# A gated linear recurrence: decay factors kept as running products instead of sums of logarithms

## The chip, the cores and the metric

One core of a Trainium2 chip runs the whole program. The metric is the device time of one execution in microseconds, the median of several runs. Five instruction queues work side by side: PE (TensorE, matrix products), DVE (VectorE), ACT (ScalarE), POOL (GpSimd) and SP (SyncE, which issues the DMA transfers). Each queue runs in order; between queues there are semaphores.

## The reference

One layer on 1024 tokens of width 1024: a forgetting attention with 8 heads, beside it a gated linear recurrence (HGRN2) with 4 heads of width 128, both projected, gated, merged and normed, then a SwiGLU network and a second norm. The change touches the recurrence alone:

```python
# f = forget gate in (0, 1), per token and channel; k = 1 - f; q = silu(...); per head
def step(state, inp):                                   # one chunk of tokens
    q_i, k_i, v_i, g_i = inp                            # g = log f
    b = jnp.cumsum(g_i, axis=2)
    o_inter = jnp.einsum('bhtd,bhde->bhte', q_i * jnp.exp(b), state)
    diff = b[:, :, :, None, :] - b[:, :, None, :, :]
    decay = jnp.exp(jnp.where(incl[None, None, :, :, None], diff, -jnp.inf))
    attn = jnp.einsum('bhtd,bhtsd,bhsd->bhts', q_i, decay, k_i)
    o_intra = jnp.einsum('bhts,bhse->bhte', attn, v_i)
    b_last = b[:, :, -1:, :]
    k_dec = k_i * jnp.exp(b_last - b)
    new_state = (jnp.exp(b_last[:, :, 0, :])[..., None] * state
                 + jnp.einsum('bhsd,bhse->bhde', k_dec, v_i))
    return new_state, o_inter + o_intra
```

The decay between tokens s and t is the product of the forget gates after s up to t, channel by channel.

## The kernel before

Everything is written as calls on five queues (`sync`, `act`, `dve`, `pool`, `pe`), which a planner (class `Plan`) collects and then puts into an order: a list scheduler with costs per instruction and 36 rounds of changed ranks. So the order on each engine, over the whole kernel, follows from the calls, the planner's costs, and the pools of tiles (`BUFS`), whose slots come free when their last user is done. Wide products are made in three passes of split float32 (`mm3`: high by high, high by low, low by high), each with 512 columns.

The stages in order of time: the value projections (`v`), the query and key projections (`qk`), attention for 8 heads (up to about 300 us), the recurrence for 4 heads (`hgrn`, about 300 to 490 us), the gate products (`gs`), the branch projections and the merge (`pps`), the output projection (`oa`, `ob`), the network (`fa` to `fe`, `p`). `hgrn_project(h + 1)` (banks `bps`) and parts of the gate products (`gate_part`, banks `ge`) need nothing of the recurrence of head h and are planned into it.

In the recurrence a tile has 128 channels by 1024 tokens. The tokens lie in windows of 128, even windows in the first half of the tile and odd ones in the second, the odd ones in reversed order, so that `place(w)` finds window w. Before, per head:

- `fk` (tile `hbf`) becomes the gate f, `k` (`hk`) is 1 - f, then f becomes log f, and eight scans sum the logarithms within each window into `b` (`hbb`); `tot` holds the sums of whole windows and `dec` their exponentials.
- `diagonal` puts the products of a token with itself into `at`, the matrix of weights.
- `level(li)`, for L = 64, 32, 16, 8, 4, 2: tokens are taken in groups of 2L; the query of a later half meets the keys of the earlier half. `e` is b minus its value at the middle (tiles of `box1`), two exponentials turn it into factors, `ke` and `qe` are key and query times their factors, four matmuls per level give `lp`, and a masked copy puts `lp` into `at`.
- `neighbours` does the same for L = 1 by products and a matmul with ones (`lp_nb`).
- `states` makes `kd` (keys decayed to the end of the window) and `qeb` (queries decayed from its start), transposes `kd` (`kdt`), multiplies with the values (`up`) and runs over the windows (`st`, in a tile called `box`).
- At the end `op` sums `at` times the values and `qeb` times the states; then the norm, the gate and the store (`ob`, `ot`, `yb`).

In names such as `lp1_0` the first figure is the head (0 to 3). In the traces such numbers are left out, and every instruction has the line of one helper (L387).

Of the kernel before, what the change touches and what calls it, by code (L numbers as in the profile page):

```python
# [12 lines left out]
ALU = mybir.AluOpType  # L13
# [377 lines left out]
def trunk(ctx: ExitStack, tc, a: dict, out: bass.AP):  # L391
# [49 lines left out]
    def f(ap):  # L441
        return ap.bitcast(F32)

    def split(hi, lo, src):
        act.copy(hi, src)
        dve.tensor_sub(lo, src, f(hi))
# [433 lines left out]
                sync.dma_start(ya_d[p, i].rearrange("a d t -> (a d) t")[:, hs(g)], y)  # L880


    once = keep([P, P + 1], "once", F32R)
    raw = half("gt", "once_r")
    sync.dma_start(raw[:, :P + 1], a["once"])
    act.copy(once, raw[:, :P + 1])
    reset, ones = f(once)[:, :P], once[:, 1:]
    lmask = const("lmask", [P, 2, MASKS], U16, "mask")
    sync.dma_start(ng, a["ng"])
    sync.dma_start(lbl, a["lbl"])  # L890
# [12 lines left out]
    def place(w):  # L903
        return blk(w % 2 * 4 + w // 2)
# [26 lines left out]
    def halves(t, L):  # L931
        return t.rearrange("p (n c l) -> p c n l", c=2, l=L)

    def hgrn(h, qfg, box):
        q, fk, sg = qfg
        k = full("kb", f"hk{h}")
        b = full("kb", f"hbb{h}")
        act.activation(fk, fk, AF.Identity, scale=olb[:, h:h + 1], bias=lb[:, h:h + 1])
        pool.tensor_scalar(k, fk, -1.0, 1.0, op0=ALU.mult, op1=ALU.add)
        act.activation(fk, fk, AF.Ln)  # L940


        bw, fw = (t.rearrange("p (c j t) -> p c j t", c=2, t=P) for t in (b, fk))
        pool.memset(bw[:, 1, :, 0:1], 0.0)
        for w in range(NT):
            o = w % 2
            dve.tensor_tensor_scan(b[:, place(w)][:, o:], reset[:, :P - o], fk[:, place(w)][:, :P - o], 0.0,
                                   op0=ALU.mult, op1=ALU.add)
        tot = small([P, 4, 2], "tot", 1)
        dve.tensor_copy(tot[:, :, 0:1], bw[:, 0, :, P - 1:P])  # L950
        dve.tensor_add(tot[:, :, 1:2], bw[:, 1, :, P - 1:P], fw[:, 1, :, P - 1:P])
        dec = small([P, NT], "dec", 1)
        act.activation(dec, tot.rearrange("p j c -> p (j c)"), AF.Exp)

        at = full("pf", f"at{h}")
        qeb = full("pf", f"qeb{h}")
        kd = full("pf", f"kd{h}")
        kdt = box[:, h % 2, :]
        st = box[:, 2 + h % 2, :]

# [3 lines left out]
        def diagonal():  # L964
            kh, kl = (full("hl", f"qk{n}{h}", F32R) for n in "hl")
            dve.tensor_mul(at, q, k)
            split(kh, kl, at)
            for hf in range(2):
                dg = bank("s", f"dg{h}_{hf}")
                for r in (kh, kl):  # L970
                    mm(dg, ones, r[:, hs(hf)], start=r is kh, stop=r is kl)
                dve.tensor_mul(at[:, hs(hf)].rearrange("p (w t) -> p w t", t=P),
                               dg.rearrange("p (w t) -> p w t", t=P), ident[:, None, :].to_broadcast([P, 4, P]))

        def level(li):
            L = LEVELS[li]
            nb = S // (2 * L)
            e = box1[:, li % 4, :]
            ev = e.rearrange("p (n a l) -> p n a l", a=2, l=L)
            bv = b.rearrange("p (n t) -> p n t", t=2 * L)  # L980
            dve.tensor_sub(e.rearrange("p (n t) -> p n t", t=2 * L), bv,
                           bv[:, :, L - 1:L].to_broadcast([P, nb, 2 * L]))
            act.activation(ev[:, :, 0, :], ev[:, :, 0, :], AF.Exp, scale=-1.0)
            act.activation(ev[:, :, 1, :], ev[:, :, 1, :], AF.Exp)
            ke = take("hl", [NB], f"ke{h}_{li}")
            qe = half("ph", f"qe{h}_{li}")
            dve.tensor_mul(halves(ke, L), across(k, L), across(e, L))
            dve.tensor_mul(halves(qe, L), across(q, L, 1), across(e, L, 1))
            lp = bank("s", f"lp{h}_{li}")
            for j in range(NT // 2):  # L990
                mm(lp[:, blk(j)], ke[:, blk(j)], qe[:, blk(j)], start=True, stop=True)
            nw = 64 // L

            if li:
                m = lmask[:, :, 4 * nw - 7:8 * nw - 7, None].to_broadcast([P, 2, 4 * nw, L])
            else:
                m = lmask[:, :, :1, None].to_broadcast([P, 2, 4, L])
            dve.copy_predicated(across(at, L, 1), m, halves(lp, L))

        def neighbours():  # L1000

            low = take("hl", [2, NB], f"nb{h}", F32R)
            hi, lo = low[:, 0, :], low[:, 1, :]
            pr, e = (half("ph", f"nb{n}{h}") for n in "pe")
            b2 = b.rearrange("p (n a) -> p n a", a=2)
            dve.tensor_sub(e, b2[:, :, 1], b2[:, :, 0])
            act.activation(e, e, AF.Exp)
            def by2(t):
                return t.rearrange("p (c n l) -> p c n l", c=2, l=1)

            dve.tensor_mul(by2(pr), across(q, 1, 1), across(k, 1))
            dve.tensor_mul(pr, pr, e)
            split(hi, lo, pr)
            lp = bank("s", f"lp{h}_nb")
            for r in (hi, lo):
                mm(lp, ones, r, start=r is hi, stop=r is lo)
            dve.copy_predicated(across(at, 1, 1).rearrange("p c (j n) l -> p c j (n l)", j=4),
                                lmask[:, :, None, MASKS - 64:].to_broadcast([P, 2, 4, 64]),
                                lp.rearrange("p (c j n) -> p c j n", c=2, j=4))

        def states():

            even, odd = hs(0), hs(1)
            for j in range(4):
                for c, t in enumerate((kd, qeb)):
                    w = blk(4 * c + j)
                    act.activation(t[:, w], b[:, w], AF.Exp, bias=tot[:, j, c:c + 1], scale=-1.0)
            act.activation(kd[:, odd], b[:, odd], AF.Exp)
            act.activation(qeb[:, even], b[:, even], AF.Exp)
            dve.tensor_mul(kd, kd, k)  # L1030
            for hf in range(2):
                tp = bank("pt", f"kdt{h}_{hf}")
                m = min(4, NT - 1 - 4 * hf)
                for w in range(m):
                    tr(tp[:, blk(w)], kd[:, place(4 * hf + w)], ident)
                act.copy(kdt[:, hf * NB:hf * NB + m * P], tp[:, :m * P])
            dve.tensor_mul(qeb, qeb, q)
            for hf in range(2):
                up = bank("pt", f"up{h}_{hf}")
                ws = range(4 * hf, min(4 * hf + 4, NT - 1))  # L1040
                for w in ws:
                    mm(up[:, blk(w % 4)], kdt[:, blk(w)], V(w), start=True, stop=True)
                for w in ws:
                    if w == 0:
                        dve.tensor_copy(st[:, blk(1)], up[:, blk(0)])
                    else:
                        dve.scalar_tensor_tensor(st[:, blk(w + 1)], st[:, blk(w)], dec[:, w:w + 1], up[:, blk(w % 4)],
                                                 op0=ALU.mult, op1=ALU.add)

        diagonal()  # L1050
        for li in range(4):
            level(li)
        states()
        for li in range(4, len(LEVELS) - 1):
            level(li)
        neighbours()

        for hf in range(2):
            op = bank("pv", f"op{h}_{hf}")
            ss, rr = (lambda t: (t[:, :4], t[:, 4:]))(small([P, 8], "ss", 3, "ss"))  # L1060
            for w in range(4):
                ww = 4 * hf + w
                mm(op[:, blk(w)], at[:, place(ww)], V(ww), start=True, stop=ww == 0)
                if ww:
                    mm(op[:, blk(w)], qeb[:, place(ww)], st[:, blk(ww)], start=False, stop=True)
            ob = half("tt", f"ob{h}_{hf}")
            for w in range(4):
                act.activation(ob[:, blk(w)], op[:, blk(w)], AF.Square, accum_out=ss[:, w:w + 1])
# [832 lines left out]
def _constants():  # L1901
# [1 line left out]
    ident = np.eye(P, dtype=np.float32)  # L1903
    causal = np.where(s[None, :] > s[:, None], np.float32(BIG), np.float32(0))
    causal = np.tile(np.concatenate([causal, causal.T], axis=1), (1, NT // 2))
    once = np.ones((P, P + 1), np.float32)
    once[:, 0] = 0
# [14 lines left out]
    return {"before": -before, "ident": ident, "causal": causal, "once": once,  # L1922
            "lmask": lmask}


# [70 lines left out]
```

## Time and profile before

| | |
|---|---|
| median of 3 runs | 1412.72 us (1412.63 to 1412.78) |
| span of the profiled execution, first to last instruction | 1410.3 us |
| median less that span (the profiled execution has no other time on record) | 2.4 us |
| PE busy, of the span | 1399.7 us, 99% |
| DVE busy | 1161.6 us, 82% |
| ACT busy | 710.5 us, 50% |
| POOL busy | 87.3 us, 6% |
| granted TensorE clock | 0.999 |

The page lists busy time by engine, then the span in 40 slices (35 us each; the recurrence is about slices 8 to 13), then groups of instructions by the tile they write and the tiles they read (`out<-in`), and waits by who released whom. A float32 matmul with 128 columns stands there as two records, one with 512 columns in split form as one.

### The profile page before, as it was taken

How to read it: one execution, taken by the hardware profiler on the slowest of the kernel's cores; microseconds unless marked ns; L12 is line 12 of the kernel's file. 1: busy time of each engine (PE TensorE's matmuls, PEld its weight loads, DVE VectorE, ACT ScalarE, POOL GpSimd, SP SyncE). 2: the span in 40 equal slices, each digit the busy share in tenths (PEclk: the TensorE clock that was granted, in tenths of full speed). 3: DMA queues.
4: the chain of work that ended last, by engine and by line, in shares of the span. 5: the costliest groups of instructions: out<-in, count | busy, mean ns of one | idle time of the engine just before them, and what ended most of it. 6: DMA issues, size and time to landing. Idle time of an engine off the chain costs nothing.

```text
span 1410.3 us, 19118 instructions
## 1 busy us (share of the span) xinstructions
PE 1399.7 (99%) x6650; PEld 1162.8 (82%) x6650; DVE 1161.6 (82%) x2025; ACT 710.5 (50%) x1275; POOL 87.3 (6%) x108
## 2 busy tenths in 40 slices
PE   9999999999999999999999999999999999999997
PEld 7788888888888888888887888888888888888886
DVE  7995878899998979778998879877687976699597
ACT  5534689887687632365439842233223334434330
POOL 0000133420000000000001000000000000000001
PEclk9999999999999999999999999999999999999999
DMA  7458999811113686456644637533334336878632
GB/s 274 156 167 271 301 291 259 243 61 45 46 53 113 215 254 196 134 165 220 231 131 140 208 103 227 181 117 100 98 106 141 112 112 209 315 249 284 216 122 90
DMA packets 99503, 245.23 MB, mean 174 GB/s; under 512 B 11456, under 2 KB 12736, under 8 KB 99408
## 3 DMA queue, kind: packets, MB, share of 16 engines
q1 hardware_dynamic: 98256, 239.83, 52.2%
q0 software_dynamic: 1152, 4.19, 1.6%
q8 instruction: 52, 0.85, 0.2%
q14 instruction: 43, 0.35, 0.1%
HBM read 181.26 MB, written 62.72 MB: 173 GB/s over the span
## 4 chain that ended last, share of the span: by engine, by line
PE 79%; DVE 1%; issue 0%; DVEq 0%
PE p L387 15%; PE fb L387 12%; PE gs L387 9%; PE fc L387 8%; PE bps L387 7%; PE fa L387 5%; PE fe L387 3%; PE pps L387 3%; PE oa L387 3%; PE ob L387 2%; PE ge L387 2%; PE lp L387 2%; PE op L387 1%; PE pv L387 1%; PE pt L387 1%; PE x1t L387 0%
## 5 line engine op out<-in xcount | busy, mean ns | idle before, releaser
L387 PE MATMUL p<-dp 128*128 128x512 f32 (+1 forms) x957 | 210.0, 382 | 0.0
L387 PEld LDWEIGHTS p<-dp 128*128 128x128 f32 x957 | 175.3, 188 | 34.8
L387 PE MATMUL fc<-xs,Tp 128*128 128x512 f32 x528 | 129.1, 389 | 0.0
L387 PE MATMUL fb<-xs,Tp 128*128 128x512 f32 x528 | 127.8, 389 | 0.0
L387 ACT CAST Tp<-t 128x512 fp32r<-128x512 f32 x88 | 54.4, 620 | 128.9 <-PE fb L387 69.1
L387 PEld LDWEIGHTS fc<-xs,Tp 128*128 128x128 f32 x528 | 99.0, 188 | 20.8 <-ACT Tp L387 0.3
L387 PEld LDWEIGHTS fb<-xs,Tp 128*128 128x128 f32 x528 | 99.1, 188 | 20.6
L387 DVE TENSOR_TENSOR Tp<-t,Tp 128x512 fp32r<-128x512 f32 x88 | 60.3, 689 | 30.9 <-ACT Tp L387 30.3
L387 PE MATMUL fa<-x,Tp 128*128 128x512 f32 x336 | 81.4, 389 | 0.0
L387 PE MATMUL bps<-xl,wb_h 128*128 128x512 f32 x192 | 77.1, 402 | 0.0
L387 PE MATMUL bps<-xh,wb_h 128*128 128x512 f32 x192 | 76.6, 401 | 0.0
L387 PE MATMUL bps<-xh,wb_l 128*128 128x512 f32 x192 | 76.2, 400 | 0.0
L387 PEld LDWEIGHTS fa<-x,Tp 128*128 128x128 f32 x336 | 63.1, 188 | 13.1
L387 ACT CAST dp<-dap 128x1024 fp32r<-128x1024 f32 (+1 forms) x42 | 41.2, 980 | 58.8 <-PE p L387 35.6
L387 POOL TENSOR_TENSOR norm<-norm,few 128x1 f32<-128x1 f32 x16 | 13.3, 830 | 902.8 <-DVE norm L387 882.9
L387 DVE TENSOR_TENSOR dp<-dap,dp 128x1024 fp32r<-128x1024 f32 (+1 forms) x42 | 47.5, 1132 | 22.4 <-ACT dp L387 22.4
L387 DVE TENSOR_TENSOR tl<-pt,th 128x512 fp32r<-128x512 f32 (+1 forms) x96 | 52.1, 551 | 8.9 <-PE pv L387 4.2
L387 PE MATMUL fb<-x,Tp 128*128 128x512 f32 x240 | 57.8, 389 | 0.0
L387 ACT CAST th<-pt 128x512 fp32r<-128x512 f32 (+1 forms) x96 | 45.4, 477 | 16.5 <-PE pt L387 9.8
L387 PEld LDWEIGHTS fb<-x,Tp 128*128 128x128 f32 x240 | 45.0, 188 | 9.4
L387 DVE TENSOR_TENSOR u<-fb,p 128x512 f32<-128x512 f32 x40 | 27.6, 690 | 22.7 <-PE fb L387 22.5
L387 PEld LDWEIGHTS bps<-xl,wb_h 128*128 128x128 f32 x192 | 36.2, 189 | 6.3
(1006 smaller groups left out, 3594.8 us busy)
## 6 DMA issues: line engine op xcount, KB each, us to landing
dbp<-in_w_fo SPq DMA_DIRECT2D x45, 512.0 KB, 4.8
dap<-a_d SPq DMA_DIRECT2D x35, 512.0 KB, 4.8
wg_r<-in_w_ff SPq DMA_DIRECT2D x22, 512.0 KB, 3.9
wu_r<-in_w_ff SPq DMA_DIRECT2D x22, 512.0 KB, 3.9
a_d<-ar SPq DMA_DIRECT2D x42, 256.0 KB, 3.0
wop_r<-in_w_o SPq DMA_DIRECT2D x18, 512.0 KB, 3.7
a_d<-as SPq DMA_DIRECT2D x33, 256.0 KB, 3.5
qk_d<-qk SPq DMA_DIRECT2D x32, 256.0 KB, 4.8
```

Of the source, the lines that this page charges most:

```text
L387: getattr(q.engine, method)(*args, **kw)
```

## The change

Logarithms, sums, differences and exponentials go. For groups of L tokens G[L] holds the product of the L gates of each group; G[1] is f itself, and G[2L] is the product of neighbours in G[L] (tile `hg`). `k` and a new tile `qf` (query times f) hold key and query already multiplied with the decay inside their group of L tokens. To go from L to 2L, `grow(L)` multiplies in place the later halves of `qf` by G[L] of the earlier half, the earlier halves of `k` by G[L] of the later half, and makes G[2L]. So the levels now run from 2 tokens upwards, `neighbours` comes first and `states` last; after `grow(64)`, `k` and `qf` are what `kd` and `qeb` were, and `dec` is G[128]. `level(L)` copies the earlier halves of `k` into `ke` on ACT, and the matmuls read the later halves of `qf` where they lie, by a strided pattern (`later_half`). The constant `once` is no longer loaded; its ones come from a memset.

```diff
-    once = keep([P, P + 1], "once", F32R)
-    raw = half("gt", "once_r")
-    sync.dma_start(raw[:, :P + 1], a["once"])
-    act.copy(once, raw[:, :P + 1])
-    reset, ones = f(once)[:, :P], once[:, 1:]
+    ones = keep([P, P], "once", F32R)
+    raw = half("gt", "once_r")[:, :P]
+    dve.memset(raw, 1.0)
+    act.copy(ones, raw)
...
+    def later_half(t, L, j):
+        return bass.AP(tensor=t.tensor, offset=t.offset + L + P * j,
+                       ap=[list(t.ap[0]), [2 * L, 64 // L], [NB - L, 2], [1, L]])
+    def spread(t, L, other=0):
+        t = across(t, 1, other)
+        dims = [list(d) for d in t.ap]
+        dims[3] = [0, L]
+        return bass.AP(tensor=t.tensor, offset=t.offset, ap=dims)
...
-        act.activation(fk, fk, AF.Ln)
-        pool.memset(bw[:, 1, :, 0:1], 0.0)
-        for w in range(NT):
-            o = w % 2
-            dve.tensor_tensor_scan(b[:, place(w)][:, o:], reset[:, :P - o], fk[:, place(w)][:, :P - o], 0.0,
-                                   op0=ALU.mult, op1=ALU.add)
...
-        qeb = full("pf", f"qeb{h}")
-        kd = full("pf", f"kd{h}")
+        qf = full("pf", f"qf{h}")
+        gs = full("kb", f"hg{h}")
+        G, o = {1: fk}, 0
+        for L in LEVELS[::-1]:
+            G[2 * L] = gs[:, o:o + S // (2 * L)]
+            o += S // (2 * L)
...
             dve.tensor_mul(at, q, k)
+            dve.tensor_mul(qf, q, fk)
...
-        def level(li):
-            L = LEVELS[li]
-            e = box1[:, li % 4, :]
-            dve.tensor_sub(e.rearrange("p (n t) -> p n t", t=2 * L), bv,
-                           bv[:, :, L - 1:L].to_broadcast([P, nb, 2 * L]))
-            act.activation(ev[:, :, 0, :], ev[:, :, 0, :], AF.Exp, scale=-1.0)
-            act.activation(ev[:, :, 1, :], ev[:, :, 1, :], AF.Exp)
-            dve.tensor_mul(halves(ke, L), across(k, L), across(e, L))
-            dve.tensor_mul(halves(qe, L), across(q, L, 1), across(e, L, 1))
+        def grow(L):
+            dve.tensor_mul(across(qf, L, 1), across(qf, L, 1), spread(G[L], L))
+            dve.tensor_mul(across(k, L), across(k, L), spread(G[L], L, 1))
+            two = G[L].rearrange("p (n a) -> p n a", a=2)
+            dve.tensor_mul(G[2 * L], two[:, :, 0], two[:, :, 1])
+        def level(L):
+            act.copy(halves(ke, L), across(k, L))
...
-                mm(lp[:, blk(j)], ke[:, blk(j)], qe[:, blk(j)], start=True, stop=True)
+                mm(lp[:, blk(j)], ke[:, blk(j)], later_half(qf, L, j), start=True, stop=True)
...
         def states():
-            for j in range(4):
-                for c, t in enumerate((kd, qeb)):
-                    w = blk(4 * c + j)
-                    act.activation(t[:, w], b[:, w], AF.Exp, bias=tot[:, j, c:c + 1], scale=-1.0)
-            act.activation(kd[:, odd], b[:, odd], AF.Exp)
-            act.activation(qeb[:, even], b[:, even], AF.Exp)
-            dve.tensor_mul(kd, kd, k)
+            dec = G[P]
...
         diagonal()
-        for li in range(4):
-            level(li)
+        neighbours()
+        grow(1)
+        for L in LEVELS[-2::-1]:
+            level(L)
+            grow(L)
         states()
-        for li in range(4, len(LEVELS) - 1):
-            level(li)
-        neighbours()
```

The planner orders the new calls anew. TensorE, head 1, the first levels before, where two groups of `lp` stand close together:

```order
L387 MATMUL kdt1_0_1023<-ident_164,kd1_1006 128x128 x4
L387 MATMUL lp1_0_1013<-qe1_0_1012,ke1_0_1011 128x128 x4
L387 MATMUL bps1_2_0_1055<-xl1_69,wb1_2_h1_1053 128x512
L387 MATMUL lp1_1_1016<-qe1_1_1015,ke1_1_1014 128x128 x4
L387 MATMUL kdt1_1_1024<-ident_164,kd1_1006 128x128 x3
```

and now, where the transposes have gone to the end and ten projections stand between the first two levels:

```order
L387 MATMUL lp1_2_1002<-qf1_992,ke1_2_1001 128x128 x4
L387 MATMUL lp1_nb_1000<-nb1_998,once_190 128x512
L387 MATMUL bps1_2_0_1035<-xh0_66,wb1_2_l0_1032 128x512
L387 MATMUL bps1_2_0_1035<-xh0_66,wb1_2_h0_1031 128x512
L387 MATMUL bps1_2_0_1035<-xl0_68,wb1_2_h0_1031 128x512
L387 MATMUL bps1_2_0_1035<-xh0_66,wb1_2_l0_1032 128x512
L387 MATMUL bps1_2_0_1035<-xh1_67,wb1_2_h1_1033 128x512
L387 MATMUL bps1_2_0_1035<-xl1_69,wb1_2_h1_1033 128x512
L387 MATMUL bps1_2_0_1035<-xh1_67,wb1_2_l1_1034 128x512
L387 MATMUL bps1_2_0_1035<-xh1_67,wb1_2_h1_1033 128x512
L387 MATMUL bps1_2_0_1035<-xl1_69,wb1_2_h1_1033 128x512
L387 MATMUL bps1_2_0_1035<-xh1_67,wb1_2_l1_1034 128x512
```

The group of the second level, `lp1_4`, is the next row after this piece. On VectorE, head 1, before, `ke` and `qe` of a level are written while another level's product is taken out:

```order
L387 TENSOR_TENSOR ke1_3_1020<-hk1_1000,box1_106 128x2x32x8
L387 TENSOR_TENSOR qe1_3_1021<-hbq1_976,box1_106 128x2x32x8
L387 COPY_PREDICATED at1_1004<-lmask_192,lp1_1_1016 128x2x8x32
L387 SCALAR_TENSOR_TENSOR yb0_1_975<-ot0_1_974,few_119,hbg0_906 128x512
L387 TENSOR_TENSOR box1_106<-hbb1_1001 128x1024
L387 COPY_PREDICATED at1_1004<-lmask_192,lp1_2_1019 128x2x16x16
```

and now, at the same levels of 8 and 16 tokens, each product grows `k` or `qf` itself, between the masked copies:

```order
L387 COPY_PREDICATED at1_991<-lmask_192,lp1_4_1004 128x2x64x4
L387 TENSOR_TENSOR hk1_990<-hk1_990,hg1_993 128x2x16x16
L387 TENSOR_TENSOR qf1_992<-qf1_992,hg1_993 128x2x32x8
L387 COPY_PREDICATED at1_991<-lmask_192,lp1_8_1006 128x2x32x8
L387 TENSOR_TENSOR hk1_990<-hk1_990,hg1_993 128x2x8x32
```

So the masked copy of a level now stands between two growths in the same queue.

More of the change, by code (lines that the diff above doesn't have):

```diff
@@ L936, in hgrn @@
         k = full("kb", f"hk{h}")
-        b = full("kb", f"hbb{h}")
         act.activation(fk, fk, AF.Identity, scale=olb[:, h:h + 1], bias=lb[:, h:h + 1])
         pool.tensor_scalar(k, fk, -1.0, 1.0, op0=ALU.mult, op1=ALU.add)
-        act.activation(fk, fk, AF.Ln)
-        bw, fw = (t.rearrange("p (c j t) -> p c j t", c=2, t=P) for t in (b, fk))
-        pool.memset(bw[:, 1, :, 0:1], 0.0)
-        for w in range(NT):
-            o = w % 2
-            dve.tensor_tensor_scan(b[:, place(w)][:, o:], reset[:, :P - o], fk[:, place(w)][:, :P - o], 0.0,
-                                   op0=ALU.mult, op1=ALU.add)
[L949 to L953, printed above, removed]
-        at = full("pf", f"at{h}")
-        qeb = full("pf", f"qeb{h}")
-        kd = full("pf", f"kd{h}")
+        at = full("pf", f"at{h}")
+        qf = full("pf", f"qf{h}")
[4 more added lines that the diff above has]
+            o += S // (2 * L)
         kdt = box[:, h % 2, :]
@@ L973, in diagonal @@
                                dg.rearrange("p (w t) -> p w t", t=P), ident[:, None, :].to_broadcast([P, 4, P]))
-        def level(li):
-            L = LEVELS[li]
-            nb = S // (2 * L)
-            e = box1[:, li % 4, :]
-            ev = e.rearrange("p (n a l) -> p n a l", a=2, l=L)
-            bv = b.rearrange("p (n t) -> p n t", t=2 * L)
-            dve.tensor_sub(e.rearrange("p (n t) -> p n t", t=2 * L), bv,
-                           bv[:, :, L - 1:L].to_broadcast([P, nb, 2 * L]))
-            act.activation(ev[:, :, 0, :], ev[:, :, 0, :], AF.Exp, scale=-1.0)
-            act.activation(ev[:, :, 1, :], ev[:, :, 1, :], AF.Exp)
-            ke = take("hl", [NB], f"ke{h}_{li}")
-            qe = half("ph", f"qe{h}_{li}")
-            dve.tensor_mul(halves(ke, L), across(k, L), across(e, L))
-            dve.tensor_mul(halves(qe, L), across(q, L, 1), across(e, L, 1))
-            lp = bank("s", f"lp{h}_{li}")
+        def grow(L):
[4 more added lines that the diff above has]
+        def level(L):
+            ke = take("hl", [NB], f"ke{h}_{L}")
+            act.copy(halves(ke, L), across(k, L))
+            lp = bank("s", f"lp{h}_{L}")
             for j in range(NT // 2):
-                mm(lp[:, blk(j)], ke[:, blk(j)], qe[:, blk(j)], start=True, stop=True)
+                mm(lp[:, blk(j)], ke[:, blk(j)], later_half(qf, L, j), start=True, stop=True)
             nw = 64 // L
-            if li:
+            if L < 64:
                 m = lmask[:, :, 4 * nw - 7:8 * nw - 7, None].to_broadcast([P, 2, 4 * nw, L])
@@ L1003, in neighbours @@
             hi, lo = low[:, 0, :], low[:, 1, :]
[L1004 to L1007, printed above, removed]
+            pr = half("ph", f"nbp{h}")
             def by2(t):
                 return t.rearrange("p (c n l) -> p c n l", c=2, l=1)
-            dve.tensor_mul(by2(pr), across(q, 1, 1), across(k, 1))
-            dve.tensor_mul(pr, pr, e)
+            dve.tensor_mul(by2(pr), across(qf, 1, 1), across(k, 1))
             split(hi, lo, pr)
@@ L1021, in states @@
         def states():
-            even, odd = hs(0), hs(1)
-            for j in range(4):
-                for c, t in enumerate((kd, qeb)):
-                    w = blk(4 * c + j)
-                    act.activation(t[:, w], b[:, w], AF.Exp, bias=tot[:, j, c:c + 1], scale=-1.0)
-            act.activation(kd[:, odd], b[:, odd], AF.Exp)
-            act.activation(qeb[:, even], b[:, even], AF.Exp)
-            dve.tensor_mul(kd, kd, k)
+            dec = G[P]
             for hf in range(2):
@@ L1034, in states @@
                 for w in range(m):
-                    tr(tp[:, blk(w)], kd[:, place(4 * hf + w)], ident)
+                    tr(tp[:, blk(w)], k[:, place(4 * hf + w)], ident)
                 act.copy(kdt[:, hf * NB:hf * NB + m * P], tp[:, :m * P])
-            dve.tensor_mul(qeb, qeb, q)
             for hf in range(2):
@@ L1046, in states @@
                     else:
-                        dve.scalar_tensor_tensor(st[:, blk(w + 1)], st[:, blk(w)], dec[:, w:w + 1], up[:, blk(w % 4)],
+                        n = w % 2 * 4 + w // 2
+                        dve.scalar_tensor_tensor(st[:, blk(w + 1)], st[:, blk(w)], dec[:, n:n + 1], up[:, blk(w % 4)],
                                                  op0=ALU.mult, op1=ALU.add)
         diagonal()
-        for li in range(4):
-            level(li)
+        neighbours()
[3 more added lines that the diff above has]
+            grow(L)
         states()
-        for li in range(4, len(LEVELS) - 1):
-            level(li)
-        neighbours()
         for hf in range(2):
@@ L1064, in hgrn @@
                 if ww:
-                    mm(op[:, blk(w)], qeb[:, place(ww)], st[:, blk(ww)], start=False, stop=True)
+                    mm(op[:, blk(w)], qf[:, place(ww)], st[:, blk(ww)], start=False, stop=True)
             ob = half("tt", f"ob{h}_{hf}")
@@ L1905, in _constants @@
     causal = np.tile(np.concatenate([causal, causal.T], axis=1), (1, NT // 2))
-    once = np.ones((P, P + 1), np.float32)
-    once[:, 0] = 0
     lmask = np.zeros((P, 2, MASKS), np.uint16)
@@ L1921, in _constants @@
     before[:, -2], before[:, -1] = 1 - 2 * (t % 2), t % 2
-    return {"before": -before, "ident": ident, "causal": causal, "once": once,
+    return {"before": -before, "ident": ident, "causal": causal,
             "lmask": lmask}
```

## The prediction

> **What bounds the kernel now.** The page's busy line comes first, then its slices.
>
> ```profile
> PE 1399.7 (99%) x6650; PEld 1162.8 (82%) x6650; DVE 1161.6 (82%) x2025; ACT 710.5 (50%) x1275; POOL 87.3 (6%) x108
> PE   9999999999999999999999999999999999999997
> DVE  7995878899998979778998879877687976699597
> ACT  5534689887687632365439842233223334434330
> ```
>
> TensorE stands at 9 in every slice. Ends of matmuls are modelled, so that alone could hide gaps; the starts are measured. In a stage that does nothing else, and in the recurrence, the timeline gives (start, us, engine, what):
>
> ```profile
> 999.65 2.88 PE L387 MATMUL fc<-xs,Tp 128*128 128x512 f32 x12
> 1002.37 1.98 PE L387 MATMUL fa<-x,Tp 128*128 128x512 f32 x8
> ...
> 470.05 0.48 PE L387 MATMUL ge<-xh,we_h 128*128 128x512 f32 x1
> 470.37 0.40 PE L387 MATMUL ge<-xl,we_h 128*128 128x512 f32 x1
> 470.60 0.40 PE L387 MATMUL ge<-xh,we_l 128*128 128x512 f32 x1
> 470.84 1.05 PE L387 MATMUL lp<-qe,ke 128*128 128x128 f32 x8
> ```
>
> Twelve 512-column matmuls start within 1002.37-999.65 = 2.72 us: 0.227 us each. In the recurrence the spacing is 0.23 too (470.37 to 470.60 to 470.84), and eight 128-column float32 records take 1.05-0.275 (the last one's own length) over 7, 0.111 us each. So TensorE issues as fast in the recurrence as where nothing disturbs it. The waits that TensorE itself had are the third view, all of them:
>
> ```profile
> PE vy L387 <- DVE few L387: 1.2, 1, 1.2
> PE vx L387 <- ACT xh L387: 0.8, 1, 0.8
> PE oa L387 <- ACT Top4h L387: 0.6, 1, 0.6
> PE s L387 <- DVE soft L387: 0.3, 1, 0.3
> PE pt L387 <- DVE tl L387: 0.3, 1, 0.3
> ```
>
> 3.2 us in 1410.3, of which 2.0 belong to the kernel's first two tiles (`vy`, `vx`) and none to a tile of the recurrence. The windows of the recurrence say who works beside it (columns: PE, PEld, DVE, ACT, POOL busy, granted clock, DMA share, GB/s):
>
> ```profile
> 300.00:350.00 50.00, 50.00 (x282) 42.81 (x281) 45.47 (x75) 40.76 (x74) 3.42 (x4) 1.00 0.17 54
> 350.00:400.00 50.00, 50.00 (x285) 43.35 (x284) 45.19 (x74) 38.99 (x86) 6.07 (x6) 1.00 0.15 48
> 400.00:450.00 50.00, 50.00 (x275) 42.98 (x274) 43.45 (x69) 37.98 (x72) 3.50 (x4) 1.00 0.20 69
> 450.00:490.00 40.00, 40.00 (x229) 34.70 (x228) 36.58 (x60) 25.79 (x58) 3.50 (x2) 1.00 0.63 211
> ```
>
> VectorE is 90% busy there (170.7 of 190) and ScalarE 76%, but TensorE fills every hole with projections of the next head (`bps`) and gate products (`ge`), which need nothing of this head.
>
> **The change part by part.** TensorE: the two orders hold the same 6474 matmuls; only operands change (`qf` for `qe` and `qeb`, `hk` for `kd`). 0 us of work, so a gain can come only out of the 1.2 us of waits behind the start, and small irregularities. I bound the gain at 2.
>
> VectorE and ScalarE, over four heads, from the groups between 290 and 495 us (busy us, mean ns):
>
> ```profile
> L387 DVE TENSOR_TENSOR box<-hbb 128x1024 f32<-128x1024 f32 x24 | 29.4, 1232 | 0.1
> L387 DVE TENSOR_TENSOR qe<-hbq,box 128x512 f32<-128x512 f32 x24 | 16.2, 686 | 0.0
> L387 DVE TENSOR_TENSOR_SCAN hbb<-once,hbf 128x128 f32<-128x128 f32 x12 | 4.8, 400 | 0.0
> L387 DVE TENSOR_TENSOR qeb<-qeb,hbq 128x1024 f32<-128x1024 f32 x4 | 4.9, 1231 | 0.3 <-ACT qeb L387 0.3
> L387 DVE TENSOR_TENSOR tl<-pt,th 128x256 fp32r<-128x256 f32 x3 | 1.3, 422 | 0.0
> L387 DVE TENSOR_TENSOR tot<-hbb,hbf 128x4 f32<-128x4 f32 x4 | 0.6, 161 | 0.0
> L387 ACT ACTIVATE box<-box 128x512 f32<-128x512 f32 x48 | 27.8, 635 | 2.0 <-DVE box L387 1.9
> L387 ACT ACT_TABLE_LOAD x13 | 16.7, 1283 | 0.2
> L387 ACT ACTIVATE kd<-hbb,tot 128x128 f32<-128x128 f32 x16 | 5.7, 400 | 0.0
> L387 ACT ACTIVATE hbf<-hbf 128x1024 f32<-128x1024 f32 x3 | 3.2, 1061 | 0.0
> ```
>
> VectorE loses the 24 differences (29.4), 32 scans (32 x 0.40 = 12.8), the products into `kd` and `qeb` (2 x 4.9), two of the neighbours' 512-element steps (8 x 0.69 = 5.5) and `tot` (8 x about 0.17 = 1.4): 58.9. It gains `qf = q*f` (4 x 1.23 = 4.9), the first level's three products (12 x 0.69 = 8.3) and the six smaller decay products per head, 256 down to 8 elements, between 0.42 and 0.16 each (24 x about 0.21 = 5): 18. The 48 products into `ke` and `qe` become 48 in-place ones of the same size: 0. Net -41 us. ScalarE loses 48 exponentials (27.8), 32 + 8 for the states (32 x 0.40 + 8 x 0.63 = 17.8), four logarithms (4 x 1.06), four neighbours' exponentials (4 x 0.63) and four small `dec` (together about 8), and 24 table loads (38 to 14 in the orders; 24 x 1.283 = 30.8); it gains 24 copies into `ke` (24 x 0.63 = 15). Net -69 us. POOL loses four memsets, SP one 66 KB load. All of it lies beside TensorE, which never waited for it: 0 us on the path. Should TensorE's filler run out under the recurrence, that cover would be gone; up to 590 us the gate products follow, independent of it.
>
> What is added is a wait. Before, each level had its own `e`, `qe` and `ke`, written ahead of the matmuls. VectorE, head 1, before (`lp1_0` is the level of 64 tokens):
>
> ```order
> L387 TENSOR_TENSOR qe1_0_1012<-hbq1_976,box1_106 128x2x4x64
> L387 TENSOR_TENSOR ke1_1_1014<-hk1_1000,box1_106 128x2x8x32
> L387 TENSOR_TENSOR qe1_1_1015<-hbq1_976,box1_106 128x2x8x32
> L387 TENSOR_TENSOR wb1_2_l1_1054<-wb1_2_r_1050,wb1_2_h1_1053 128x512
> L387 TENSOR_TENSOR qe1_2_1018<-hbq1_976,box1_106 128x2x16x16
> L387 TENSOR_TENSOR ke1_2_1017<-hk1_1000,box1_106 128x2x16x16
> L387 COPY_PREDICATED at1_1004<-lmask_192,lp1_0_1013 128x2x4x64
> ```
>
> Three levels are ready before the first result is taken. Now `qf` is overwritten in place, so level 2L cannot be made before level L's matmuls have read it. The same engine and head, after:
>
> ```order
> L387 TENSOR_TENSOR qf1_992<-qf1_992,hg1_993 128x2x128x2
> L387 COPY_PREDICATED at1_991<-lmask_192,lp1_nb_1000 128x2x256
> L387 TENSOR_TENSOR hk1_990<-hk1_990,hg1_993 128x2x64x4
> L387 COPY_PREDICATED at1_991<-lmask_192,lp1_2_1002 128x2x128x2
> L387 TENSOR_TENSOR hk1_990<-hk1_990,hg1_993 128x2x32x8
> L387 TENSOR_TENSOR qf1_992<-qf1_992,hg1_993 128x2x64x4
> ```
>
> Between the growth that frees `lp1_4` and the one that frees `lp1_8` stand four other steps. TensorE has between those two matmul groups, after:
>
> ```order
> L387 MATMUL lp1_4_1004<-qf1_992,ke1_4_1003 128x128 x4
> L387 MATMUL bps1_2_0_1035<-xh1_67,wb1_2_h1_1033 128x512
> L387 MATMUL bps1_2_0_1035<-xl1_69,wb1_2_h1_1033 128x512
> L387 MATMUL bps1_2_0_1035<-xh1_67,wb1_2_l1_1034 128x512
> L387 MATMUL bps1_2_0_1035<-xh1_67,wb1_2_h1_1033 128x512
> L387 MATMUL bps1_2_0_1035<-xl1_69,wb1_2_h1_1033 128x512
> L387 MATMUL bps1_2_0_1035<-xh1_67,wb1_2_l1_1034 128x512
> L387 MATMUL ge14_1194<-xl0_68,we14_h0_1190 128x512
> L387 MATMUL ge14_1194<-xh0_66,we14_l0_1191 128x512
> L387 MATMUL lp1_8_1006<-qf1_992,ke1_8_1005 128x128 x4
> ```
>
> Eight fillers, in a queue that cannot pass a waiting `lp`; all projections behind it wait too. VectorE's pace there is read from its starts:
>
> ```profile
> 470.49 0.72 DVE L387 COPY_PREDICATED at<-lmask,lp 128x512 f32<-128x512 uint16 x1
> 471.10 0.68 DVE L387 TENSOR_TENSOR we_l<-we_r,we_h 128x512 fp32r<-128x512 f32 x1
> 471.70 0.72 DVE L387 COPY_PREDICATED at<-lmask,lp 128x512 f32<-128x512 uint16 x1
> ...
> 473.43 1.31 DVE L387 COPY_PREDICATED at<-lmask,lp 128x512 f32<-128x512 uint16 x1
> 474.53 0.33 DVE L387 COPY box<-up 128x128 f32<-128x128 f32 x1
> 474.85 1.31 DVE L387 COPY_PREDICATED at<-lmask,lp_nb 128x512 f32<-128x512 uint16 x1
> 475.95 0.32 DVE L387 SCALAR_TENSOR_TENSOR box<-box,dec,up 128x128 f32<-128x128 f32 x1
> ```
>
> A 512-element product takes 0.60 of the queue, a masked copy 0.61, but 1.10 for the level of two tokens (473.43) and the neighbours. So VectorE needs 1.10 + 0.60 + 1.10 + 0.60 + 0.69 (the last to its end) = 4.1 us; TensorE brings 4 x 2 x 0.111 + 8 x 0.227 = 2.7. It is 1.4 us short, unless it comes to `lp1_4` that much later than it could. Reckoned the same way, head 0 is 1.5 short, head 2 0.3, head 3 not at all. The sum, 3.2 us, is the upper bound; the lower is 0, since before, with VectorE fuller, no such wait reached TensorE. I take 0.8, nearer to the waits shown.
>
> The strided operand is the other unseen cost: `later_half` reads runs of L elements where `qe` was contiguous, and the trace has no strided moving operand. Bound below 0. Above: the masked copy at runs of two costs 1.10/0.61 = 1.8 times that at longer runs; applied to the 16 matmuls of two-token runs, 16 x 2 x 0.111 x 0.8 = 2.8 us. The product groups at the same runs (`qe`, 24 of all levels at a mean of 686) show no such jump, and they only read and write SBUF as TensorE's read does: I take 0. A second argument: a float32 record takes 0.87 ns a column, the 512-column ones 0.44, so the slow one leaves room.
> [...]
>
> Sum, against the profiled execution's span of 1410.3 (the median of the runs, 1412.7, lies 2.4 above it, start and end of the launch): 0 of work, +0.8 for the chain, 0 for strides, 0 for relief of VectorE and ScalarE: 1411.1 + 2.4, about 1413.4.
>
> **The rivals.** A measurement here can tell about 0.2%, 2.8 us, from no change.
> The chain binds in full (slower): TensorE reaches each `lp` as soon as the growth before it ends, and the missing time of heads 0 to 2 shows: 1412.7 + 3.2 = 1415.9. For it: the deficits above; against: a spread of fillers that also differs by head. It decides once TensorE's lead at `lp_4` is below 1.4 us.
> The strided read costs (slower): at runs of two 1412.7 + 2.8 + 0.8 = 1416.3; if all 96 matmuls ran at 1.8 times, 96 x 2 x 0.111 x 0.8 = 17, 1430.
> A transfer comes late: SP's order differs from the attention on, where DMA is full,
>
> ```profile
> 225.00:250.00 25.00, 25.00 (x151) 21.61 (x149) 20.91 (x68) 22.68 (x50) 11.10 (x15) 1.00 0.97 265
> 250.00:275.00 25.00, 25.00 (x159) 21.95 (x158) 21.96 (x78) 20.04 (x50) 9.81 (x14) 1.00 1.02 300
> ...
> wg_r<-in_w_ff SPq DMA_DIRECT2D x22, 512.0 KB, 3.9
> ```
>
> and one load of q, k or a weight block late by a whole landing (3.9 us in the last row) would give 1416.6. Against: the bytes are the same.
> The relief does count (faster): if TensorE's busy time hid the recurrence's pace, up to the 41 us of VectorE could come off, 1372. The spacing of 0.23 within it speaks against.
>
> **How the numbers follow.** Unchanged within 0.2%: 0.71. Chain in full 0.10, strided read 0.07, late transfer or another new wait 0.07: slower 0.24. Faster 0.05, most of it for waits that I can't see. The time is the likeliest case, 1413.4; its own range is 1411 (2 us of waits gone) to 1415.5. The range of 1411.0 to 1417.5 takes in the chain, the two-token read and a late transfer, and leaves out the wide strided case and the large gain.
>
> **What would show it.** Right: TensorE's list of waits stays under 5 us, with at most a microsecond on `lp` behind `qf`; VectorE near 1120 us, ScalarE near 640, 14 table loads, `lp` records still 0.111 apart. Wrong: `lp` records of the two-token level spaced wider, `lp<-qf` leading the waits with over 2.5 us, or TensorE idle in the attention.

## The result: slower by 8.9 us, and the profile after

The changed kernel takes 1421.62 us (median, 1419.83 to 1421.80) beside 1412.75 us before (1412.63 to 1413.41): ratio 1.006, 95% interval 1.0046 to 1.0074. The forecast was 1413.4, within 1411.0 to 1417.5, and it was wrong. The page of the changed kernel begins so (span 1420.0 us, 1410.3 before):

```profile
PE 1404.2 (99%) x6650; PEld 1163.8 (82%) x6650; DVE 1134.4 (80%) x1986; ACT 649.2 (46%) x1175; POOL 87.3 (6%) x104
PE   9999989999999999999999999999999999999997
```

The instructions of TensorE are as many as before, VectorE is busy for 27 us less and ScalarE for 61. TensorE still shows 99%, but one slice, the sixth (counted from 1; 178 to 213 us), has fallen to 8. That is the attention, more than 100 us ahead of the recurrence's first `lp` at 332.6 us. The waits of TensorE, all of them:

```profile
PE pv L387 <- ACT th L387: 3.4, 1, 3.4
PE s L387 <- DVE soft L387: 1.4, 1, 1.4
PE vy L387 <- DVE idle L387: 1.2, 1, 1.2
PE pt L387 <- DVE sums L387: 0.7, 1, 0.7
PE fe L387 <- ACT ep L387: 0.5, 1, 0.5
PE oa L387 <- DVE Top4l L387: 0.4, 1, 0.4
PE vx L387 <- ACT xh L387: 0.4, 1, 0.4
PE ge L387 <- ACT ge L387: 0.3, 1, 0.3
```

Against the five rows of before, `pv` behind `th` is new and `s` behind `soft` has grown from 0.3 to 1.4; both belong to the attention. No row names a tile of the recurrence. The same stretch in the windows (columns as in the prediction: PE, PEld, DVE, ACT, POOL busy, granted clock, DMA share, GB/s), first before:

```profile
175.00:200.00 25.00, 24.73 (x137) 20.57 (x136) 17.18 (x54) 20.89 (x42) 10.03 (x12) 1.00 1.04 308
```

and after:

```profile
175.00:200.00 25.00, 21.65 (x111) 17.81 (x110) 15.94 (x56) 17.89 (x36) 10.54 (x13) 0.93 0.89 261
```

26 matmuls fewer in 25 us, and the clock granted to TensorE was 0.93, not 1.00. To follow such losses through a run I added up, over all matmul starts, by how much each start comes later after the one before it than matmuls of the same sizes do in the trace of before (their median). I call the sum TensorE's lag; it is worked out from the traces (us, at six moments of the span). Its level depends on how finely the sizes are told apart, by several us late in the span; the differences between the two kernels hardly do:

```
                             150     225     300     475     775    1375
before                       2.6     3.3     4.0     5.1     6.6     6.1
after                        2.6    10.4    12.0    13.7    15.6    16.1
e1  new math, old order      2.5     3.9     4.3     6.7     9.0     8.6
e10 after, ten loads later   2.9     3.9     5.4     7.1     9.1     9.5
```

Of the 10.0 us between the two kernels at the end (the two spans differ by 9.7), 7.1 arise from 150 to 225 us (10.4 - 2.6 less 3.3 - 2.6), 0.9 from 225 to 300, 0.6 under the recurrence (300 to 475), 1.4 later. Other ways to tell the sizes apart put the 7.1 at 6.9 to 7.2. So most of the time was not lost where the code was changed.

What happened at 182 us stands in the timeline. ScalarE's rows of `th` (the high half of the attention's weights, head 0), the fourth after 3.71 us of waiting for a store of a query:

```profile
171.94 0.59 ACT L387 CAST th<-pt 128x512 fp32r<-128x512 f32 x1 [0.66 <-PE pt L387]
175.12 0.48 ACT L387 CAST th<-pt 128x384 fp32r<-128x384 f32 x1
177.14 0.37 ACT L387 CAST th<-pt 128x256 fp32r<-128x256 f32 x1 [0.80 <-DVE tl L387]
185.67 0.27 ACT L387 CAST th<-pt 128x128 fp32r<-128x128 f32 x1 [3.71 <-DMA qk_d<-qk]
```

`th` has nothing to do with that query; both tiles come from the pool `tt`, which has four slots, and the wait in the trace is for the store's landing: `th` takes over a slot that the store still holds. SP's queue says why it landed late:

```profile
173.43 1.42 SPq L387 DMA_DIRECT2D k<-qk_d  x2
175.56 1.25 SPq L387 DMA_DIRECT2D kl<-qk_d  x2
176.90 1.38 SPq L387 DMA_DIRECT2D qk_d<-qk  x2
```

and the chain that ended last runs right through it (start, us, what; rows left out at the dots):

```profile
168.67 7.67 DMA kl<-qk_d
...
176.90 8.70 DMA qk_d<-qk
...
185.99 0.47 PE pv L387
...
193.63 9.83 DMA box<-nf_d
```

The store was issued behind four loads of head 2's keys (1 MB), which TensorE first used at 200 us, in full DMA queues (DMA share 1.02 from 180 to 185 us), and took 8.7 us. Behind the pause TensorE ran slowly:

```profile
187.79 0.63 PE L387 MATMUL ge<-xl,we_h 128*128 128x512 f32 x1
188.21 0.63 PE L387 MATMUL ge<-xh,we_l 128*128 128x512 f32 x1
188.64 0.41 PE L387 MATMUL s<-k,q 128*128 128x256 f32 x1
```

0.42 to 0.43 us from start to start and not 0.23; the granted clock was 0.50 in every half microsecond from 186.5 to 189 us. So one late store cost 3.5 us of pause (by the lag) and 1.5 of half speed; 1.6 came with the wait of `s` at 204 us, for the mask in `box`, whose transfer took 9.8 us (the last row of the chain).

### The profile page after: what moved, and what is told of

The parts are those of the page before. It is cut to its first block, busy times and chain, and to the rows that moved or that the text cites. A ratio compares the mean times of both kernels' runs of the same rounds, so it can differ in the third digit from the quotient of the medians.

```text
span 1420.0 us, 19016 instructions
## 1 busy us (share of the span) xinstructions
PE 1404.2 (99%) x6650; PEld 1163.8 (82%) x6650; DVE 1134.4 (80%) x1986; ACT 649.2 (46%) x1175; POOL 87.3 (6%) x104
## 4 chain that ended last, share of the span: by engine, by line
PE 96%; DMA 2%; DVE 1%; ACT 1%; issue 0%; SPq 0%; POOL 0%; DVEq 0%; ACTq 0%; POOLq 0%
PE p L387 15%; PE fb L387 12%; PE bps L387 9%; PE gs L387 8%; PE fc L387 8%; PE fa L387 5%; PE vx L387 4%; PE oa L387 3%; PE pps L387 3%; PE fe L387 3%; PE qk_s L387 3%; PE qk_h L387 2%; PE ob L387 2%; PE vy L387 2%; PE pv L387 2%; PE pt L387 2%
## 5 line engine op out<-in xcount | busy, mean ns | idle before, releaser
L387 POOL TENSOR_SCALAR p<-p,sums 128x128 f32<-128x128 f32 (+7 forms) x48 | 34.5, 730 | 127.3 <-PE qk_h L387 65.8
```

The costliest lines, as they stand in the source:

```text
L387: getattr(q.engine, method)(*args, **kw)
```

## The experiments

The edit touched one function; the planner then wrote a new order for the whole program. Theory P: the new order outside the recurrence costs the time. Theory R: the new recurrence does. In the four kernels of the first comparison the two are taken apart; `before` was 1412.84 there. "Ranks" are the numbers by which the planner picks the next call.

**e1, the new recurrence in the old order.**

```diff
     def improve(self, slack, wait):
-        ...
+        self.turn = self.rank = RANKS   # calls outside the recurrence: those that before ended with
+        return self.schedule(slack, wait)
```

> The changed recurrence, but every call outside it (9611 of 10156) takes the rank that the planner ended with in the kernel before; the recurrence's own calls keep their ranks of the changed kernel, put on the same scale; one pass of the planner instead of 36. Theory P (the 9 us come from the planner's other order outside the recurrence, above all in the attention between 150 and 225 us, where transfers come late): 1412 to 1415 us, and TensorE's waits on th and soft near 180 and 204 us are gone. Theory R (the new recurrence itself is slower: chained levels, copies, decay products): 1419 to 1422.

Measured 1414.43 us (1413.42 to 1417.22), ratio 1.0009 (1.0000 to 1.0019): 1.6 us, at the edge of what can be told. Ranks do not pin the order wholly: counted by tile names in the traces, 5823 of TensorE's 6198 matmuls outside the recurrence stand in the place that they had before, where of the changed kernel's 4622 do. All its waits:

```profile
PE vy L456 <- DVE idle L456: 1.2, 1, 1.2
PE oa L456 <- ACT Top4h L456: 0.6, 1, 0.6
PE gs L456 <- DVE gu L456: 0.3, 1, 0.3
PE s L456 <- DVE soft L456: 0.3, 1, 0.3
```

**e2, the old recurrence in the new order** (the same edit in `before`, with the ranks of after).

> The reverse: the recurrence of before with logarithms, and every call outside it at the rank it ended with in the changed kernel. Theory P: 1418 to 1423 us, with the late transfers near 180 us back. Theory R: 1412 to 1415.

Measured 1422.46 us (1418.90 to 1423.98), ratio 1.0064 (1.0046 to 1.0082), with the very wait at the head of its list:

```profile
PE pv L457 <- ACT th L457: 3.6, 1, 3.6
PE gs L457 <- DVE gu L457: 1.4, 1, 1.4
```

Theory R falls: the old arithmetic is as slow in the new order as the new one, and the new is within 1.6 us of the old in the old order.

**e3 and e4, another draw of the planner for each kernel.**

```diff
-        vary = np.random.default_rng(1)
+        vary = np.random.default_rng(2)
```

> The kernel before with one edit: the planner's random numbers start from 2 instead of 1, so that its rounds try other ranks. Theory P: several us slower than before, 1415 to 1422, since the order of before was one good draw. Theory R says nothing on it, but if orders hardly matter: 1412 to 1414.

> The changed kernel with the planner's random numbers started from 2. Theory P: any place between 1412 and 1424, several us from 1421.6, as likely nearer to before as not. Theory R: within 2 us of 1421.6.

e3 (`before`) took 1416.79 us (ratio 1.0026, 1.0016 to 1.0035), e4 (after) 1420.54 (1.0057, 1.0037 to 1.0076). A new seed alone costs the old kernel 4 us. In e4 the waits are others (`bps` 2.4 us, `pv` behind `ya` 1.7): the slot of `th` was one accident of several that an order can have.

**e5 and e6, spliced orders** (each kernel's order written out, and what comes before 225 us taken from the other), to see whether the start of the attention is all.

> The new recurrence; what the two orders share and what stands before 225 us in them (projections, start of the attention) is in the order of before, everything later exactly in the order of after. Theory P1 (the loss is one of the attention's start, 150 to 225 us, where the changed kernel's TensorE falls 7.1 us behind the old one): before's lag up to 225 us (3.3 us) plus after's growth from there on (16.0 - 10.4 = 5.6) is 8.9 us against 6.0 of before, so 1412.8 + 2.9 = 1415.7, range 1414.5 to 1417. Theory P2 (the re-ordering costs a little everywhere): most of the loss stays, 1418 to 1421. Theory R (the recurrence itself): 1421.

> The mirror of the run before: the old recurrence, what is shared and stands before 225 us in the order of after, everything later exactly in the order of before. Theory P1: after's lag up to 225 us (10.4) plus before's growth from there on (6.0 - 3.3 = 2.7) is 13.1 against 6.0, so 1412.8 + 7.1 = 1419.9, range 1418.5 to 1421, with a wait of some 3 us of pv on th near 185 us. Theory P2: 1414 to 1417. Theory R: 1412.8.

e5 took 1427.96 us (ratio 1.0110, 1.0095 to 1.0125), e6 1426.91 (1.0098, 1.0083 to 1.0113); `before` was 1413.07. Both expectations missed by 7 to 12 us: a spliced order has waits of its own on both sides of the seam, ahead of it in e5 (`bps` behind `hbf`, 3.3 us in two waits) and behind it in e6 (the same wait, 1.4 us at 227 us). e6 does carry the wait of `pv` on `th` (3.1 us at the longest) into the old recurrence. As a measure of the stretch before 225 us the two are of no use; they show how much an order that no planner made can cost.

**e7, one cause taken away.** The changed kernel in its own order, but for four calls on SP:

```diff
-k2_2, k2_2, kl_2, kl_2 <- qk_d
 qk_d <- qk3_010
 qk_d <- qk3_101
 box1 <- in_causal
 a21_3 <- in_xT
 qk_d <- qk3_011
+k2_2, k2_2, kl_2, kl_2 <- qk_d
```

> The changed kernel with its own order, but for four calls: the loads of k and kl of head 2 (1 MB, first needed at about 203 us) are issued on SP behind the stores of the last query half (qk_d from qk3_010 and qk3_011) and not ahead of them. Theory P1 with one wait as its main part (th of head 0 gets the slot of that store's tile; the store lands late because those loads stand ahead of it in full DMA queues): the 3.4 us wait of pv on th near 185 us falls under 1 us and the three half-speed matmuls behind it go too, so 1421.6 - 3.4 - 0.6 = 1417.6, range 1416.3 to 1419. Theory P2 or a rival in which the lateness is only passed on (the DMA queues are full, so the next transfer is late instead: box at 203 us, or head 2's keys): 1420 to 1422.

The store went out 1.0 us earlier and `th` waited for nothing:

```profile
175.90 0.79 SPq L493 DMA_DIRECT2D qk_d<-qk  x2
```

```profile
181.38 0.26 ACT L493 CAST th<-pt 128x128 fp32r<-128x128 f32 x1
```

From issue to landing the stores of `qk_d` issued from 174 to 182 us took half as long as in the changed kernel. That kernel's two (this view starts the count some 0.4 us later than the chain does):

```profile
DMA to landing us min/median/max: 8.3/8.3/8.3
```

and e7's three:

```profile
DMA to landing us min/median/max: 4.1/4.2/4.3
```

TensorE's list lost the 3.4 us and kept 1.5 of `s` behind `soft`; the profiled execution spans 1414.4 us, 5.6 less than after's. The median says less, 1419.33 (1416.16 to 1423.55, ratio 1.0055, 1.0036 to 1.0074): its executions differ by 7 us, the longest two at a mean clock of 0.996, the shortest at 0.999. So some of them ran for longer at a lower clock; where in the run, no trace shows.

**e10, a second cause taken away:** e7, and six loads of head 3 (`q2_3`, `k2_3`, `kl_3`, 1.5 MB) moved on SP behind that head's loads of `box`.

> e7 and one move more: the six loads of q, k and kl of head 3 (1.5 MB) are issued on SP behind the loads of causal and nf_d for that head, so that they no longer fill the DMA queues while POOL's accumulating load of nf_d for head 2 is on its way. If waits of this kind add up one by one: the 1.4 to 1.8 us wait of s on soft near 200 us goes, and with e7's undisturbed execution (1416.2 us) the time is 1414.7, range 1413.5 to 1416.5. Rival (the lateness is passed on to the next transfer in full queues): 1416 to 1420, with a wait of s on a load of head 3 near 215 us.

1415.70 us (1414.66 to 1420.04; ratio 1.0025, 1.0015 to 1.0034; `before` 1412.71 there), and its list has neither of the two waits:

```profile
PE vy L492 <- DVE idle L492: 1.2, 1, 1.2
PE pt L492 <- DVE sums L492: 0.7, 1, 0.7
PE fe L492 <- ACT ep L492: 0.5, 1, 0.5
PE oa L492 <- DVE Top4l L492: 0.5, 1, 0.5
PE ge L492 <- ACT ge L492: 0.3, 1, 0.3
```

Ten DMA issues in another place give back 5.9 of 8.9 us; in the traces the instructions of TensorE, VectorE, ScalarE and GpSimd stand in the very sequence of the changed kernel. So the two late transfers together are shown as a cause. How the 5.9 us divide between them is not: e7's executions scatter too far. TensorE's listed waits now come to 3.2 us, as much as before's, and the 3.0 us that remain have no wait to show for them.

**e8 and e9, is the planner's idea of slots to blame?** The planner lets a tile take the slot that it reckons free first; the pool hands slots out in the turn in which the program gave them up. For `th` of head 0 that was the suspicion; the slot that the plan had reckoned with is not on record.

```diff
-                        t = max(t, sorted(slots[tag])[k][0] + 60)
+                        t = max(t, slots[tag][k][0] + 60)
...
-                old = min(s)
-                s.remove(old)
+                old = s.pop(0)
```

> The new recurrence, re-seeded as in e4 (1420.5 us), with one thing more: the planner takes a pool's slot in the turn in which the slots were given up in the program, as the pool itself does, and no longer the slot that it reckons free first. Theory S (the re-planning of the changed kernel loses time because the planner counts on another slot than the tile gets, as for th of head 0, which got the slot of a qk_d store still on its way): waits of TensorE on a tile whose slot is held by a store go, 1414 to 1417. Rival P3 (any new order meets some 4 to 8 us of waits of its own, whatever the planner knows of slots, and the order of before was a lucky one): 1417 to 1421, with other waits at the head of TensorE's list.

> The kernel before with the same two-line change to the planner and nothing else. Theory S: about as before or a little better or worse, 1411.5 to 1415. Rival P3: this is a new order like e2 and e3, 1416 to 1421. Under both the recurrence itself is the old one.

The new recurrence went from e4's 1420.54 to 1415.80 us (1414.68 to 1417.72; ratio 1.0021, 1.0012 to 1.0030), as that theory wanted, but `before` with the same edit went from 1412.71 to 1420.45 (ratio 1.0051, 1.0036 to 1.0066). The second speaks for the rival; the first alone would have misled me.

**e11 and e12, a version to beat both:** the new recurrence with slots in turn and orders from a far longer search than the planner's 36 rounds (of the search only the orders that it found are on record).

> A version meant to be the best: the new recurrence in an order found by a much longer search (about 5000 trials of changed ranks, started from the order of e1, slots in turn as in e8). If the order is all that stands between the two kernels, a good order brings the new recurrence to the time of before or under it: 1411 to 1414, with TensorE's waits under 4 us. If the new recurrence itself costs something that an order can't hide (the chain of in-place levels, 0.6 to 1.3 us of lag in e1 and e10): 1413.5 to 1416. If a searched order has its own unforeseen waits again (as in e9): 1416 to 1420.

> The same search with other random trials from another start, as a second draw: how much of e11's time is luck. With the theory that a long search does it, within 1.5 us of e11; with the theory that each order brings waits of its own that the planner doesn't foresee, anywhere from 1412 to 1420.

1420.98 us (1419.17 to 1422.95; ratio 1.0053, 1.0040 to 1.0066) and 1417.58 (1416.23 to 1419.29; 1.0030, 1.0019 to 1.0041); `before` 1412.84. e11 waits for things that no earlier order waited for:

```profile
PE qk_pv L508 <- DVE Tqk1p2l L508: 2.1, 1, 2.1
```

Neither beats even e1: a longer search by the planner's own costs did not bring an order that the chip runs better. Nor do listed waits explain it: e12's come to 4.3 us, 1.1 more than before's, and it takes 4.7 us more. The orders in one table, without e5, e6 and e7 (us; the first two rows say what the arithmetic is worth):

```
order                        old recurrence   new recurrence
that of before               1412.8           1414.4
that of after                1422.5           1421.6
another seed                 1416.8           1420.5
slots in turn (e9; e8)       1420.5           1415.8
long search                                   1421.0, 1417.6
after's, ten loads later                      1415.7
```

At about equal order the new recurrence is 1.6 slower and 0.9 faster: nothing that can be told. The order of before is the best of all that were measured, 3 to 9 us better than the seven other draws of a planner (after, e3, e4, e8, e9, e11, e12), and an edit that makes the planner draw again stands to lose that. Whether that order was itself the best of several that had been timed is not on record; if it was, a loss on the next draw was to be expected. Why one order runs so much better than another, beyond the two waits taken away in e7 and e10, stays open.

## Why the prediction was wrong, step by step

**0 us of work on TensorE:** right, 6650 matmul records on both pages.

**Relief of VectorE and ScalarE on nobody's path:** right. VectorE came to 1134.4 (forecast near 1120), ScalarE to 649.2 (near 640), the table loads to 14, and in the old order (e1) none of it shortened anything. 4.9 of VectorE's 14 us are the small decay products, counted at 5 us and measured at 9.9 (below). Most of the rest is a matter of counting: instruction by instruction VectorE lost 36.0 us (forecast 41) and ScalarE 71.0 (69), but the page counts time in which two neighbouring instructions overlap once, and by it they lost 27.2 and 61.3.

**The in-place chain, 0.8 us within 0 to 3.2:** not contradicted. TensorE's list has no wait on `lp`. The lag grows under the recurrence (300 to 475 us) by 1.7 us in after, 1.7 in e10 and 2.4 in e1, against 1.1 before: 0.6 to 1.3 more, but the old recurrence in e9's order grew by 2.5, so even this is no more than an order does. That VectorE needed 4.1 us where TensorE brought 2.7 did not matter; it was `ke` on ScalarE and VectorE that waited:

```profile
  ACT ke L387: 6.9, 7
  DVE at L387: 5.3, 3
  DVE qf L387: 2.0, 6
```

(who waited for `lp`, how long in all, how often).

**The strided operand, 0 us within 0 to 2.8:** right but for 0.3. Groups of eight `lp` records, the first at runs of two elements, the others at 4 and 8:

```profile
332.63 1.13 PE L387 MATMUL lp<-qf,ke 128*128 128x128 f32 x8
336.84 1.05 PE L387 MATMUL lp<-qf,ke 128*128 128x128 f32 x8
339.79 1.05 PE L387 MATMUL lp<-qf,ke 128*128 128x128 f32 x8
```

0.08 us more in each of four heads, and nothing from runs of four on. Runs of two have a price of 7% (0.120 us a record, 0.111 to 0.112 at longer runs), where the prediction's upper bound had 80%. The wide case, all 96 matmuls at 1.8 times, did not come: runs of four to 64 cost nothing.

**The step that failed: "A transfer comes late", chance 0.07, price one landing, 3.9 us, dismissed with "the bytes are the same".** The kind of cause was right, SP's order in the attention with DMA full, and of the prediction's signs of being wrong it was "TensorE idle in the attention" that came. The path was not foreseen: no load that a matmul reads, but a store that kept a tile's slot, and then the load of a mask. The size was wrong: the store's landing took 8.7 us and the mask's 9.8, two waits came, the longer one drew slow matmuls behind it, and the lag grew by 7.1 us more than before's. The 3.9 us were the row of a load in the network; before's own trace had the price of this stretch (issues from 165 to 215 us, the last figure the median us to landing):

```profile
qk_d<-qk SPq DMA_DIRECT2D x6, 256.0 KB, 6.7
box<-nf_d POOLq DMA_DIRECT2D x2, 512.0 KB, 8.9
```

And the chance was wrong, because the forecast counted what the edit does to the recurrence and set the re-drawing of thousands of other calls at 0 but for one late load; the spread of such draws, 1416 to 1422 us here, was the number to ask for. With five waits of 3.2 us in all, before could hardly gain by a new draw and could easily lose.

## What to carry to other kernels

Where a search writes the order of a whole program, an edit is two changes: what it does, and a new draw. Measure them apart, with the old order pinned on the new code and with a re-seeded old kernel, before giving the arithmetic a price or a merit. And where a tile is given up by a store, look at what stands ahead of that store in its queue and who gets the slot next.

## What the runs showed of the hardware

**The longest pauses of TensorE had a low clock behind them.** After, from 185 to 190 us, behind the pause of 3.4, the granted clock (third number from the right) was 0.66:

```profile
185.00:190.00 5.00, 4.01 (x16) 3.56 (x17) 1.16 (x5) 3.61 (x8) 1.39 (x3) 0.66 0.99 320
```

With the 0.50 of 186.5 to 189 us as the low clock (matmuls 0.42 to 0.43 us apart and not 0.23), 0.34 x 5 / 0.5 is 3.4 us of it; the lengths that follow are reckoned in the same way. e5 has a stretch of the same length (0.04 + 0.30 of two 5 us windows, 3.4 us) behind pauses of only 1.1 and 2.3 us with 0.6 us of work between them:

```profile
195.00:200.00 5.00, 2.49 (x9) 1.74 (x10) 2.25 (x3) 3.17 (x5) 2.04 (x2) 0.96 1.03 253
200.00:205.00 5.00, 5.00 (x22) 3.99 (x21) 0.69 (x1) 1.39 (x2) 0.90 (x1) 0.70 1.05 376
```

In e6 3.4 us follow a pause of 3.1 (clock 0.83 from 183 to 193 us), in e2 twice that length, 6.8, one of 3.6 (0.55 and 0.77 from 185 to 190 and to 195 us). Shorter pauses alone show no low clock: 2.4 us in e4 (1.00, below), 2.1 in e11 (1.00 in each of six stretches from 20 to 1400 us), 1.4 at 203 us in the changed kernel (1.00 in each microsecond from 202 to 206).

```profile
178.00:186.00 8.00, 5.63 (x32) 4.41 (x31) 5.07 (x18) 5.36 (x15) 3.61 (x6) 1.00 1.01 333
```

So a low clock stood behind single pauses of 3.1 to 3.6 us and, in e5, behind a mostly idle stretch of two shorter ones. Why it stood for 3.4 us, or twice that, no run shows.

**Some products of VectorE took longer beside GpSimd's scalings.** Head 0's small decay products, of 256, 128 and 64 elements, run beside three of POOL's scalings:

```profile
289.25 2.75 DVE L387 TENSOR_TENSOR hg<-hg 128x256 f32<-128x256 f32 x3
```

```profile
289.05 2.88 POOL L387 TENSOR_SCALAR p<-p,sums 128x640 f32<-128x640 f32 x3 [1.85 <-DVE sums L387]
```

0.88, 0.88 and 0.92 us, whatever their size; in head 1, with POOL idle, 0.46, 0.28 and 0.22:

```profile
337.86 0.46 DVE L387 TENSOR_TENSOR hg<-hg 128x256 f32<-128x256 f32 x1
340.03 0.28 DVE L387 TENSOR_TENSOR hg<-hg 128x128 f32<-128x128 f32 x1
343.03 0.22 DVE L387 TENSOR_TENSOR hg<-hg 128x64 f32<-128x64 f32 x1
```

Not each one took longer: head 0's product of 32 elements, at 292.52 us, took 0.18 beside a scaling that ran from 292.51 to 293.70. What decides it, no run shows. The forecast's 0.21 us for each lies between rows of before at 0.42 (`tl`, 256 elements) and 0.16 (`tot`); five of those seven ran with POOL idle.
